# A four-layer encoder in split fp32r on one Trainium2 core: the first projections take low-rank and value columns of four feature tiles together, and of four apart

## The chip, the core and the metric

The kernel runs on one core of one Trainium2 chip, as one program with one launch. The metric is the device time of that program in microseconds, the median of several executions. The engines that matter are TensorE (PE for matmuls, PEld for the loading of their stationary operands), VectorE (DVE), ScalarE (ACT), GpSimd (POOL) and SyncE, whose queue (SPq) issues nearly all transfers from device memory.

## The reference

The input is one sequence of 256 tokens with 1024 features. Layer 0 has two groups of heads behind one input projection, and only this projection is touched by the change:

```python
def even_mixer(xn, w_in, rpb, q_norm, w_uq, kv_norm, w_ukv, w_o, cos_r, sin_r):
    hcat = xn @ w_in                       # 1024 -> 512 q, 512 k, 512 v, 256 c_q, 128 c_kv, 32 k_pe
    a_qkv = hcat[..., :o0].reshape(b, s, 3, NA_HEADS, HEAD_DIM)
    out_a = neighbourhood_attention(a_qkv[:, :, 0], a_qkv[:, :, 1], a_qkv[:, :, 2], rpb)
    c_q = rms_norm(hcat[..., o0:o1], q_norm)
    c_kv = rms_norm(hcat[..., o1:o2], kv_norm)
    k_pe = apply_rope(hcat[..., o2:][:, :, None, :], cos_r, sin_r)
    q = (c_q @ w_uq).reshape(...)          # second stage of the low-rank heads
    kv = (c_kv @ w_ukv).reshape(...)
    out_b = dense_attention(q, k, v, (MLA_NOPE + MLA_ROPE) ** -0.5)
    return jnp.concatenate([out_a, out_b], axis=-1) @ w_o

for layer in range(2):
    xn = rms_norm(x, norm_mix[layer])
    x = x + (even_mixer if layer == 0 else odd_mixer)(xn, ...)
    x = x + square(relu(rms_norm(x, norm_mlp[layer]) @ w1)) @ w2
return rms_norm(x, norm_final)
```

Layer 1 has dilated-window attention, and each layer ends in an MLP with 4096 hidden features. All arithmetic is fp32.

## The kernel before, in words

**Three passes for a product.** TensorE multiplies in fp32r, and each operand is cut into a high and a low half: `split` casts to the high half on ACT (L173) and takes the difference as the low half on DVE (L174). A product is then three matmuls, high by high, high by low and low by high (`mm3`, L177 to L179). All weights pass through this: `load_weight` brings a raw tile of up to 1 MB by SPq into one of four buffers (`raw`), `split_piece` cuts a quarter of it into `whi` and `wlo` (three buffers each), and `weight()` hands the halves to a product while it asks for four loads and two splits ahead.

**The input.** `x` holds the features transposed: eight feature tiles (`KT`) of 128 features on the partitions, 256 tokens beside. `prepare(k, ...)` multiplies tile `k` with its gain and cuts it into the pair `xh`, `xl` (ACT L213, DVE L214). The division by the norm is left until behind the products: `square_steps` (L220 to L224) sums squares, `rstd` turns them by one matmul (`columns`, L231), an addition on DVE (`ms`, L233) and a power on POOL (L239) into one factor for each token, and `diagonal` spreads it.

**The first products (`even`).** In the beginning SPq alternates a piece of `x` (128 KB) with a piece of the low-rank weights `w_c` (208 KB, 416 columns of one feature tile), eight times; then come three pieces of `w_v` (512, 512 and 1024 KB, the value columns), two 1 MB tiles of `w_qk` (queries and keys of two heads each), four small tables for the rotation and the low-rank gains (`small_loads`), and the rest. PE first runs eight matmuls on zeros (`keep_warm`), and then:

- the low-rank products of all eight feature tiles `k` for both token tiles `t`, 48 matmuls of 416 columns into two accumulators `pc` (`c_product`);
- the value products, first tiles 0 to 3 of both token tiles, then tiles 4 to 7, 48 matmuls of 512 columns (`v_steps`), with `columns` between;
- the first query and key product `qk_steps(0)` (48 matmuls of 256 columns), in the middle of it `as_row`, which lays the token factors along a row;
- `turn_c[0]`, three transposes of the normalised low-rank rows `cn` of token tile 0 (L516); the first quarter of `qk_steps(1)`; `turn_c[1]`, the same for token tile 1; the rest of `qk_steps(1)`.

`c_tail` makes those `cn`: sums of squares on ACT (L504), then for each of the two parts `ss` (L505), a power on POOL (`rsqrt`, L204), a product (L507) and the scaling (L508). The stretch up to the value products stands in the order in which it is written (`manual_schedule`); what follows is ordered by the scheduler of the tile framework.

**Attention of layer 0.** A list of main steps (the query and key products 1 to 3, the second low-rank stage, the output projection) is woven with the steps of the attention: `scores(n)` (L186 for the first group), the softmax (`sn` and its minimum `mn` on DVE, L677; the exponential on ACT, L682; the reciprocal, L683; the scaling, L685), `turn_probs` (transposes, L692) and `mix` (L706). Each of the first eight `scores` adds a bias of 256 KB (`load_bias`, two buffers), so a bias can be fetched only when the softmax two steps before has read its own.

Of the kernel before, what the change touches and what calls it, by code (L numbers as in the profile page):

```python
# [44 lines left out]
def trunk(ctx, tc, a, out):  # L45
# [32 lines left out]
    x = act.tile([P, KT, T], F32, name="x")  # L78
# [38 lines left out]

    plan("w_c", 4 * 416)
# [16 lines left out]
    def load_weight(pieces=1, before=lambda i: None):  # L135
        j = state["loaded"]
        src, n = specs[j]
        raw = wraw.tile([P, WCH], F32, tag="raw", name="raw")
        for i in range(pieces):
            c = cut(j, i, pieces)  # L140
            before(i)
# [316 lines left out]
    def even(ep):  # L458
        xT = xh, xl, _ = pair_tile()
        for j in range(2):  # L460
            load_weight(4, lambda i: nc.sync.dma_start(x[:, 4 * j + i, :], a["x"][:, 4 * j + i, :]))
        load_weight(2)
        load_weight()
# [6 lines left out]
        def small_loads():  # L470
# [3 lines left out]
            nc.sync.dma_start(gc[:, 256:384], a["kv_norm"].partition_broadcast(P))  # L474

# [16 lines left out]
        def c_product(pc, wc, k, t):  # L492
            wh, wl = wc
            ws = slice((k % 4) * 416, (k % 4) * 416 + 416)
            mm3(pc[:, 0:416], xh[:, k, tok(t)], xl[:, k, tok(t)], wh[:, ws], wl[:, ws], k == 0, k == KT - 1)

        def c_tail(t, pc):
            rt = column(r, t)
            cn = scratch([384], "cn")
            for c0, c1, tg in ((0, 256, "q"), (256, 384, "c")):  # L500
                n = c1 - c0
                ss = work.tile([P, 1], F32, tag="ss" + tg, name="ss")
                junk = scratch([n], "junk")
                nc.scalar.activation(junk, pc[:, c0:c1], AF.Square, scale=rt, accum_out=ss)  # L504
                nc.vector.tensor_scalar(ss, ss, 1.0 / n, EPS, ALU.mult, ALU.add)  # L505
                rc = rsqrt(ss, tg)
                nc.vector.tensor_tensor(rc, rc, rt, op=ALU.mult)  # L507
                nc.vector.scalar_tensor_tensor(cn[:, c0:c1], pc[:, c0:c1], rc, gc[:, c0:c1], ALU.mult, ALU.mult)  # L508
# [11 lines left out]
        def v_steps(t):  # L520
            hold = []

            def step(ks):
                if not hold:
                    hold.append(bank("acc"))
                for k in ks:
                    if t == 0 and k % 4 == 0:
                        wv.append(weight())
                    wh, wl = wv[k // 4]
                    ws = slice((k % 4) * 512, (k % 4) * 512 + 512)  # L530
                    mm3(hold[0], xh[:, k, tok(t)], xl[:, k, tok(t)], wh[:, ws], wl[:, ws], k == 0, k == KT - 1)
                return hold[0]
            return step

# [3 lines left out]
        wc, wv = [], []  # L538
        pc = [bank("acc") for _ in range(NT)]
        s = sum_tile()  # L540
        with tc.manual_schedule(engines={ENG.PE, ENG.Activation, ENG.DVE}):
            for k in range(KT):
# [4 lines left out]
                if k % 4 == 0:  # L547
                    wc.append(parts[k // 4][1:])
                for t in range(NT):
                    c_product(pc[t], wc[k // 4], k, t)  # L550
            state["used"] = 2
            del parts[0], parts[1]
            ins = [split_piece() for _ in range(WPARTS)][-1]
# [493 lines left out]
```

## Time and profile before

| what | value |
|---|---|
| median of 3 runs (lowest, highest) | 758.24 us (757.81, 758.55) |
| the profiled execution: its time | 758.64 us |
| the profiled execution: span of its records | 756.9 us |
| PE busy | 747.0 us (99%) |
| PEld busy | 688.3 us (91%) |
| DVE busy | 524.8 us (69%) |
| ACT busy | 512.7 us (68%) |
| POOL busy | 9.9 us (1%) |
| mean DMA rate over the span | 171 GB/s |
| first matmul on data starts at | 4.73 us |
| first query and key product starts at | 28.26 us |

How to read it: all times of the profile are in microseconds from the start of the span, "mean ns" is of one instruction. Matmuls are pipelined, so their durations overlap: what a matmul costs PE is the distance from its start to the next start, not its duration. A line of the timeline gives the start, the duration (of the whole group, where it says x2 or more), the engine, the source line, the operation, output and inputs with shapes, and in brackets the idle time of that engine before it with what ended it. "waits" sums such idle times: who waited, for whom, us in total, times, longest.

### The profile page before, as it was taken

The numbers are of one execution on the slowest core, as the hardware profiler recorded it, in microseconds if no ns is written. First come the engines' busy times: TensorE is split into PE (matmuls) and PEld (weight loads), VectorE is DVE, ScalarE is ACT, GpSimd is POOL, SyncE is SP. The second block draws the span as 40 slices with busy tenths as digits, with TensorE's granted clock in tenths as the row PEclk, the third lists the DMA queues.
The fourth block names the chain that finished last, engine by engine and source line by source line (L and its number), as shares of the span: only waits on it lengthen the run. The fifth ranks groups of instructions, "written<-read, shape, count | busy, mean of one in ns | idle before, by whom it ended". The sixth has DMA issues, their size and how long they took to land.

```text
span 756.9 us, 13681 instructions
## 1 busy us (share of the span) xinstructions
PE 747.0 (99%) x5386; PEld 688.3 (91%) x5386; DVE 524.8 (69%) x1091; ACT 512.7 (68%) x1111; POOL 9.9 (1%) x22
## 2 busy tenths in 40 slices
PE   8999999999999999999999999999999999999996
PEld 6888899999999999999999999999998888888885
DVE  5878858856656657886686677776759766566664
ACT  6779966545445545888989889889967554554551
POOL 0100000000000001000000000000000000000000
PEclk9999999999999999999999999999999999999998
DMA  8854334555455544643444444434554464554501
GB/s 299 293 209 155 112 112 146 189 193 185 179 186 187 185 148 179 224 153 125 162 161 154 154 139 168 155 139 158 219 196 167 166 223 167 178 211 171 192 29 55
DMA packets 22816, 129.08 MB, mean 171 GB/s; under 512 B 2912, under 2 KB 5472, under 8 KB 9824
## 3 DMA queue, kind: packets, MB, share of 16 engines
q1 hardware_dynamic: 22464, 127.94, 47.4%
q8 instruction: 42, 0.69, 0.4%
q10 hardware_dynamic: 288, 0.28, 0.1%
q14 instruction: 22, 0.18, 0.1%
HBM read 127.16 MB, written 1.05 MB: 169 GB/s over the span
## 4 chain that ended last, share of the span: by engine, by line
PE 90%; DVE 3%; DMA 2%; issue 1%; ACT 1%; POOL 1%; SPq 1%; POOLq 0%; DVEq 0%
PE acc L177 19%; PE acc L179 19%; PE acc L178 19%; PE w L341 16%; PE w L342 8%; DVE wlo L174 2%; PE w L881 1%; PE w L186 1%; PE w L861 1%; DMA raw<-in_w_v 1%; PE w L692 1%; PE w L706 1%; DMA bias<-in_rpb 1%; PE acc L891 1%; DMA raw<-in_w_c 1%
## 5 line engine op out<-in xcount | busy, mean ns | idle before, releaser
L174 DVE TENSOR_TENSOR wlo<-raw,whi 128x512 fp32r<-128x512 f32 (+3 forms) x488 | 307.5, 663 | 145.7 <-ACT whi L173 145.3
L173 ACT CAST whi<-raw 128x512 fp32r<-128x512 f32 (+3 forms) x488 | 266.2, 601 | 143.7 <-PE w L341 61.7
L341 PE MATMUL w<-pair,whi 128*128 128x512 f32 x512 | 181.3, 395 | 0.0
L342 PE MATMUL w<-pair,wlo 128*128 128x256 f32 x512 | 143.2, 280 | 0.0
L177 PE MATMUL acc<-pair,whi 128*128 128x256 f32 x432 | 125.4, 290 | 0.0
L179 PE MATMUL acc<-pair,wlo 128*128 128x256 f32 x432 | 121.9, 282 | 0.0
L178 PE MATMUL acc<-pair,whi 128*128 128x256 f32 x432 | 121.4, 281 | 0.0
L341 PEld LDWEIGHTS w<-pair,whi 128*128 128x128 f32 x512 | 96.1, 188 | 22.3
L342 PEld LDWEIGHTS w<-pair,wlo 128*128 128x128 f32 x512 | 96.1, 188 | 0.5
L177 PEld LDWEIGHTS acc<-pair,whi 128*128 128x128 f32 x432 | 81.1, 188 | 1.3 <-issue 0.3
L178 PEld LDWEIGHTS acc<-pair,whi 128*128 128x128 f32 x432 | 81.9, 189 | 0.0
L179 PEld LDWEIGHTS acc<-pair,wlo 128*128 128x128 f32 x432 | 81.2, 188 | 0.0
L179 PE MATMUL acc<-hh,wlo 128*128 128x256 f32 x256 | 72.4, 283 | 0.0
L177 PE MATMUL acc<-hh,whi 128*128 128x256 f32 x256 | 72.4, 283 | 0.0
L178 PE MATMUL acc<-hl,whi 128*128 128x256 f32 x256 | 72.4, 283 | 0.0
L177 PE MATMUL acc<-whi,pair 128*128 128x384 f32 (+2 forms) x160 | 56.4, 352 | 0.5 <-ACT whi L173 0.5
L178 PE MATMUL acc<-wlo,pair 128*128 128x384 f32 (+2 forms) x160 | 55.4, 346 | 0.4 <-DVE wlo L174 0.3
L179 PE MATMUL acc<-whi,pair 128*128 128x384 f32 (+2 forms) x160 | 55.0, 344 | 0.0
L177 PEld LDWEIGHTS acc<-hh,whi 128*128 128x128 f32 x256 | 49.0, 191 | 0.6
L179 PEld LDWEIGHTS acc<-hh,wlo 128*128 128x128 f32 x256 | 49.0, 191 | 0.0
L178 PEld LDWEIGHTS acc<-hl,whi 128*128 128x128 f32 x256 | 49.0, 191 | 0.0
L177 PE MATMUL acc<-whi,hh 128*128 128x512 f32 x122 | 47.9, 393 | 0.0
(207 smaller groups left out, 1247.7 us busy)
## 6 DMA issues: line engine op xcount, KB each, us to landing
raw<-in_w SPq DMA_DIRECT2D x64, 1024.0 KB, 4.8
raw<-in_w_oqk SPq DMA_DIRECT2D x24, 1024.0 KB, 4.8
raw<-in_w_ov SPq DMA_DIRECT2D x16, 768.0 KB, 4.3
raw<-in_w_qk SPq DMA_DIRECT2D x4, 1024.0 KB, 10.1
raw<-in_w_oe SPq DMA_DIRECT2D x4, 1024.0 KB, 6.9
raw<-in_w_oo SPq DMA_DIRECT2D x4, 1024.0 KB, 4.8
bias<-in_rpb SPq DMA_DIRECT2D x8, 256.0 KB, 4.7
raw<-in_w_c SPq DMA_DIRECT2D x8, 208.0 KB, 4.3
```

What stands on the lines that cost most here:

```text
L173: a = nc.scalar.copy(hi, src).ins
L174: return a, (eng or nc.vector).tensor_tensor(lo, src, hi.bitcast(F32), op=ALU.subtract).ins
L177: nc.tensor.matmul(o, sh, mh, start=first, stop=False)
L178: nc.tensor.matmul(o, sh, ml, start=False, stop=False)
L179: nc.tensor.matmul(o, sl, mh, start=False, stop=last)
L186: nc.tensor.matmul(o[j], y[pb, 0, ts], z[pb, 1, :], start=n == 0, stop=n == 2)
L341: nc.tensor.matmul(two(pu[f]), w[0][:, c], xT[2][:, k], start=k == 0, stop=False)
L342: nc.tensor.matmul(pu[f][:, 0:T], w[1][:, c], xT[0][:, k, :], start=False, stop=k == KT - 1)
L692: nc.tensor.transpose(pt[:, b * P:(b + 1) * P], pp[:, b // 2, (b % 2) * P:(b % 2 + 1) * P], ident)
L706: nc.tensor.matmul(pvo[64 * j:64 * j + 64, 0:P], v[:, kk, h * 64:(h + 1) * 64], pts[:, 2 * j + kk, :], start=kk == 0, stop=kk == NT - 1)
L861: nc.tensor.matmul(ss[i][j][rows, T:T + P], d["q12"][:, j, i * P + 64 * c:i * P + 64 * c + 64], d["k12"][:, j, 2 * i + c, :], start=True, ...
L881: nc.tensor.transpose(pt[:, b * P:(b + 1) * P], pp[:, b * P:(b + 1) * P], ident)
```

## The change

- **Layout of the weights and of x.** The low-rank and value columns of feature tiles 0 to 3 are joined in one array `w_cv` (two tiles of two features, 928 columns each); `w_c` and `w_v` keep feature tiles 4 to 7. The gains, before a transfer of their own on ACT's queue, stand ahead of `x` in one array `gx`.
- **Transfers.** The first ones on SPq are now `gx` with the gains and tile 0 (144 KB), `w_cv` 416 columns (208 KB), `w_cv` 512 columns (256 KB), `x` tile 1, again 208 and 256 KB, `x` tiles 2 and 3 together (256 KB), `w_cv` of features 2 and 3 in pieces of 464 KB, `x` 4 and 5, `w_c` of 4 and 5 (416 KB), `x` 6 and 7, `w_c` of 6 and 7. The four small tables come next, ahead of `w_v` (two halves of 512 KB) and of the four tiles of `w_qk`.
- **Order of the products.** Feature tiles 0 to 3: 6 matmuls of 416 columns and then 6 of 512 columns for each. Tiles 4 to 7: 6 matmuls of 416 columns. Then the values of tiles 4 to 7, token tile 0 and then token tile 1. For tile 0 both token tiles take one pass after another. Four accumulators (two `pc`, two `pv`) are open at once. The numbers of matmuls and their shapes stay.
- **Splits.** They are cut along the pieces. For tile 0 the high half of the low-rank columns is copied on DVE, not on ACT. The squares are summed within the loop. The splits of `w_v` and of the first `w_qk` follow directly behind (`split_piece` eight times), ahead of the norm's factors.
- **c_tail.** The two parts share one `ss`, one power and one product; the factor `1/n` goes into a scale `rs` for each part.
- **keep_warm** has seven matmuls, not eight.

```diff
-    keep_warm(8)
-    gains = const.tile([P, 4 * KT], F32, name="gains")
-    nc.scalar.dma_start(gains, a["gains"])
+    keep_warm(7)
...
-        for j in range(2):
-            load_weight(4, lambda i: nc.sync.dma_start(x[:, 4 * j + i, :], a["x"][:, 4 * j + i, :]))
-        load_weight(2)
-        load_weight()
+        load_weight((0, 416, CV, CV + 416, 2 * CV), lambda i: load_x(i // 2) if i % 2 == 0 else None)
+        load_weight((0, CV, 2 * CV), lambda i: load_x(2, 2) if i == 0 else None)
+        load_weight((0, 2 * 416, 4 * 416), lambda i: load_x(4 + 2 * i, 2))
...
+        small_loads()
+        load_weight((0, WCH // 2, WCH))
+        load_weight()
...
+            ss = work.tile([P, 2], F32, tag="ssc", name="ss")
+            for i, (c0, c1) in enumerate(cuts):
+                nc.scalar.activation(junk, pc[:, c0:c1], AF.Square, scale=rs[:, i, t:t + 1], accum_out=ss[:, i:i + 1])
+            nc.vector.tensor_scalar(ss, ss, EPS, None, ALU.add)
+            nc.gpsimd.tensor_tensor(rc, ss, mhalf.broadcast_to([P, 2]), op=ALU.pow)
+            nc.vector.tensor_scalar(rc, rc, rt, None, ALU.mult)
...
             for k in range(KT):
                 upper, lower = prepare(k, 0, xT)
                 upper()
-                lower()
-                split_piece()
...
+                if k == 0:
+                    nc.vector.tensor_copy(wc[1], wc[0])
+                    lower()
+                    nc.vector.tensor_tensor(wc[2], wc[0], wc[1].bitcast(F32), op=ALU.subtract)
+                else:
+                    lower()
+                    split(wc[1], wc[2], wc[0])
+                if wv:
+                    split(wv[1], wv[2], wv[0])
+                if k in (3, 5, 6, 7):
+                    squares.pop(0)()
+                for w, ps_, n in ((wc, pc, 416), (wv, pv, 512)):
+                    if w is not None:
+                        for passes in ((0,), (1,), (2,)) if k == 0 else (range(3),):
+                            for t in range(NT):
+                                product(ps_[t], n, w, k, t, passes)
+            state["split"] = 3 * WPARTS
+            for i in range(2 * WPARTS):
                 split_piece()
...
+            for t in range(NT):
+                for k in range(4, KT):
+                    product(pv[t], 512, [z[:, k - 4] for z in wv], k, t)
+                    if (t, k) == (0, 5):
+                        r = rstd(s)
```

The written order shows in three places. The first is SPq behind the pieces of the low-rank weights, where the small tables and the next weights stand. Before:

```order
L142 DMA raw<-in_w_c 128x416
L142 DMA raw<-in_w_v 128x1024 x2
L142 DMA raw<-in_w_v 128x2048
L142 DMA raw<-in_w_qk 128x2048 x2
L471 DMA cosr<-in_cos_r 128x64
L472 DMA sinr<-in_sin_r 128x64
L473 DMA gc<-in_q_norm 128x256
L474 DMA gc<-in_kv_norm 128x128
L142 DMA raw<-in_w_qk 128x2048 x2
```

And now:

```order
L84 DMA gx<-in_gx 128x512
L148 DMA raw<-in_w_cv 128x928 x2
L84 DMA gx<-in_gx 128x512
L148 DMA raw<-in_w_c 128x832
L84 DMA gx<-in_gx 128x512
L148 DMA raw<-in_w_c 128x832
L476 DMA cosr<-in_cos_r 128x64
L477 DMA sinr<-in_sin_r 128x64
L478 DMA gc<-in_q_norm 128x256
L479 DMA gc<-in_kv_norm 128x128
L148 DMA raw<-in_w_v 128x1024 x2
L148 DMA raw<-in_w_qk 128x2048 x4
```

The four tables moved ahead of `w_v` and of all `w_qk`, and the pieces ahead of them are larger and fewer.

The second place is DVE behind the first token tile's `c_tail`, up to the rows `cn` of token tile 1 that `turn_c[1]` transposes. `wlo_396` (before) and `wlo_379` (now) are the low halves of the second `w_qk`, `wlo_478` and `wlo_461` those of the third. Before:

```order
L505 TENSOR_SCALAR ss_352<-ss_352 128x1
L507 TENSOR_TENSOR rstd_356<-rstd_356,rstd_290 128x1
L508 SCALAR_TENSOR_TENSOR cn_351<-acc_133,rstd_356,gc_128 128x256
L174 TENSOR_TENSOR wlo_478<-raw_301,whi_477 128x512 x2
L505 TENSOR_SCALAR ss_360<-ss_360 128x1
L507 TENSOR_TENSOR rstd_364<-rstd_364,rstd_290 128x1
L508 SCALAR_TENSOR_TENSOR cn_351<-acc_134,rstd_364,gc_128 128x128
```

And now:

```order
L180 TENSOR_TENSOR wlo_379<-raw_372,whi_378 128x512
L515 TENSOR_SCALAR ss_347<-ss_347 128x2
L180 TENSOR_TENSOR wlo_461<-raw_374,whi_460 128x512
L518 TENSOR_SCALAR rstd_353<-rstd_353,rstd_294 128x2
L520 SCALAR_TENSOR_TENSOR cn_346<-acc_133,rstd_353,gc_118 128x256
L520 SCALAR_TENSOR_TENSOR cn_346<-acc_133,rstd_353,gc_118 128x128
```

Two rounds of `ss`, power and product became one, and one low half of the third `w_qk` stands ahead of `cn`, not two. Between `ms` and this `cn` there were ten low halves of `w_qk` before, four of them of the first tile; now there are five, since the first tile's four stand ahead of `ms`.

The third place is DVE at the first softmax, whose `sn` reads the first bias and so lets the third bias be fetched. `wlo_573` (before) and `wlo_556` (now) are the low halves of the fourth `w_qk`. Before:

```order
L174 TENSOR_TENSOR cl_130<-w_500,ch_129 128x3x128
L174 TENSOR_TENSOR wlo_573<-raw_393,whi_572 128x512 x4
L585 TENSOR_TENSOR q32_544<-acc_487,both_125 128x512
L677 ISA sn_559,mn_560<-w_550,bias_418 128x256
L677 ISA mn_560 128x1
L677 ISA sn_559,mn_560<-w_551,bias_418 128x256
L677 ISA mn_560 128x1
L174 TENSOR_TENSOR qk_l_543<-q32_544,qk_h_542 128x512
```

And now:

```order
L180 TENSOR_TENSOR cl_129<-w_483,ch_128 128x3x128
L608 TENSOR_TENSOR q32_527<-acc_470,both_115 128x512
L700 ISA sn_542,mn_543<-w_533,bias_401 128x256
L700 ISA mn_543 128x1
L700 ISA sn_542,mn_543<-w_534,bias_401 128x256
L700 ISA mn_543 128x1
L180 TENSOR_TENSOR qk_l_526<-q32_527,qk_h_525 128x512
L180 TENSOR_TENSOR wlo_556<-raw_376,whi_555 128x512
L706 RECIPROCAL rz_545<-z_544 128x2
L180 TENSOR_TENSOR wlo_556<-raw_376,whi_555 128x512 x3
```

The four low halves moved from ahead of the first `sn` to behind it. On SPq the fetch of the third bias stands one place earlier too, ahead of the second tile of the output weights and no longer behind it.

More of the change, by code (lines that the diff above doesn't have):

```diff
@@ L138, in load_weight @@
         raw = wraw.tile([P, WCH], F32, tag="raw", name="raw")
[L139 to L141 removed]
+        edges = edges or (0, n)
+        for i, c in enumerate(slice(*e) for e in zip(edges, edges[1:])):
+            earlier(i)
             nc.sync.dma_start(raw[:, c], src[:, c])
@@ L570, in even @@
+            dg = [diagonal(r, t) for t in range(NT)]
+            turn_c = [c_tail(t, pc[t]) for t in range(NT)]
+            state["used"] = 4
+            for j in range(4):
+                del parts[j]
+            for t in range(NT):
+                v_out(t, pv[t])
         qk = {}
```

95 lines of the change are left out of this document (39 added, 56 removed).

## The prediction, as put on record

> **What bounds the kernel now.** I read the page's first line, then the waits of TensorE over the whole span:
>
> ```profile
> PE 747.0 (99%) x5386; PEld 688.3 (91%) x5386; DVE 524.8 (69%) x1091; ACT 512.7 (68%) x1111; POOL 9.9 (1%) x22
> ...
> PE w L186 <- DVE obl L174: 0.6, 1, 0.6
> PE acc L177 <- ACT whi L173: 0.5, 1, 0.5
> PE w L692 <- ACT pp L685: 0.5, 1, 0.5
> PE w L516 <- DVE cn L508: 0.4, 1, 0.4
> PE acc L178 <- DVE wlo L174: 0.3, 2, 0.2
> ```
>
> TensorE is the bound, and its waits look small. But matmuls overlap, so idle time hides inside modelled durations. The timeline of PE, read by starts, shows more; the stretch is the one the change rewrites:
>
> ```profile
> 1.19 3.59 PE L87 MATMUL acc<-warm 128*128 128x512 bf16 x8 [1.19 <-DVE warm L82]
> 4.73 0.71 PE L177 MATMUL acc<-whi,pair 128*128 128x416 f32 x1
> ...
> 7.08 0.45 PE L177 MATMUL acc<-whi,pair 128*128 128x416 f32 x1 [0.51 <-ACT whi L173]
> 7.70 0.45 PE L178 MATMUL acc<-wlo,pair 128*128 128x416 f32 x1 [0.17 <-DVE wlo L174]
> ...
> 9.31 0.35 PE L177 MATMUL acc<-whi,pair 128*128 128x416 f32 x1
> ...
> 11.56 0.35 PE L177 MATMUL acc<-whi,pair 128*128 128x416 f32 x1
> ...
> 16.23 0.40 PE L177 MATMUL acc<-whi,pair 128*128 128x512 f32 x1
> ...
> 18.69 0.39 PE L177 MATMUL acc<-whi,pair 128*128 128x512 f32 x1
> ...
> 21.50 0.39 PE L177 MATMUL acc<-whi,pair 128*128 128x512 f32 x1
> ...
> 28.26 0.28 PE L177 MATMUL w<-pair,whi 128*128 128x256 f32 x1
> ```
>
> From 9.31 to 11.56 lie 12 matmuls of 416 columns: 0.188 us each, so 48 need 9.0. They take 11.5 (4.73 to 16.23): 2.5 us idle. From 18.69 to 21.50 lie 12 of 512 columns: 0.234 each, so 48 need 11.2. They take 12.0 (16.23 to 28.26); of the 0.8 left I put half to the column matmuls, which stay, and half to waits. What they wait for shows on ACT, which casts as the pieces land:
>
> ```profile
> 4.87 0.51 ACT L213 ACTIVATE pair<-x,gains 128x256 fp32r<-128x256 f32 x1 [0.20 <-DMA x<-in_x]
> 6.49 0.54 ACT L173 CAST whi<-raw 128x416 fp32r<-128x416 f32 x1 [1.11 <-DMA raw<-in_w_c]
> ...
> 11.36 0.54 ACT L173 CAST whi<-raw 128x416 fp32r<-128x416 f32 x1
> ...
> 13.94 0.54 ACT L173 CAST whi<-raw 128x416 fp32r<-128x416 f32 x1 [0.95 <-DMA raw<-in_w_c]
> ```
>
> These are tile 1 of x (480 KB asked for so far, the gains included), and the low-rank pieces of tiles 1, 6 and 7 (688, 2368 and 2704 KB). So pieces land at (2368 - 688)/4.87 = 345 KB/us at best and (2704 - 688)/7.45 = 271 KB/us with the late last one. A low-rank tile brings 336 KB for 1.13 us of PE, some 300 KB/us: as much as lands, so every late piece is idle time. With its values a tile brings 592 KB for 2.53 us, 234 KB/us. That is what the regrouping alters. The last view is of windows (busy time of PE, PEld, DVE, ACT, POOL, clock, share of the transfer engines, GB/s), for the queue and for the load of DVE and ACT:
>
> ```profile
> 14.00:15.00 1.00, 0.98 (x4) 0.37 (x2) 0.49 (x1) 0.48 (x1) 0.00 (x0) 1.00 1.05 434
> 22.00:23.00 1.00, 1.00 (x8) 0.91 (x7) 1.00 (x3) 1.00 (x3) 0.00 (x0) 1.00 1.04 285
> 23.00:24.00 1.00, 1.00 (x6) 0.82 (x5) 1.00 (x3) 0.99 (x2) 0.00 (x0) 1.00 0.92 187
> 24.00:25.00 1.00, 1.00 (x6) 0.77 (x6) 0.10 (x2) 0.06 (x1) 0.71 (x1) 1.00 1.02 165
> 80.00:90.00 10.00, 10.00 (x85) 8.91 (x85) 9.27 (x31) 9.82 (x29) 0.00 (x0) 1.00 0.29 107
> ```
>
> **The change part by part.** *Tile 0.* Its first matmul can start only when `whi` exists. The copy on DVE runs beside ACT's pair, and seven warm-up matmuls of 0.44 us end by about 4.3, so the start moves from 4.73 to between 4.2 and 4.8. This is worth nothing by itself, because the values of tile 0 gate the next six matmuls: they are the 608th KB, between 480 KB (4.87) and 688 KB (6.49), so 5.9. Cast 0.6, six matmuls 1.4: tile 0 ends at 7.9. The low half is done by 7.1, ahead of its pass.
>
> *Tile 1.* Low-rank weights at 944 KB: 6.49 + 256/345 = 7.2, cast by 7.8, in time for 7.9. With the low half late by 0.2, as at 7.70, PE ends at 7.9 + 2.53 + 0.2 = 10.65.
>
> *Tile 2.* Its weights are one piece of 464 KB that must land whole, at 1920 KB: 6.49 + 1232/345 = 10.1 or, by the slower rate, 11.0. With 0.6 for the cast, PE starts at 10.65 to 11.6. I take 10.95, nearer to the fast rate, because rows of 2 KB and more move faster than the 1 and 1.6 KB ones now (434 GB/s at 14, when rows of 4 and 8 KB of `w_v` move).
>
> *The rest of the products.* From tile 2 on PE needs 12 x 0.188 + 12 x 0.234 + 24 x 0.188 + 24 x 0.234 = 15.2, the column matmuls 0.4 and a late low half 0.2: 15.8. So the first query product starts at 26.7 (26.4 to 27.4) instead of 28.26: **1.5 us won (0.85 to 1.85)**.
>
> *DVE, which must follow.* These rows are of DVE, POOL and one of PE:
>
> ```profile
> 9.53 0.48 DVE L214 SCALAR_TENSOR_TENSOR pair<-x,gains,pair 128x256 fp32r<-128x256 f32 x1
> 10.46 0.48 DVE L214 SCALAR_TENSOR_TENSOR pair<-x,gains,pair 128x256 fp32r<-128x256 f32 x1
> 15.97 2.57 DVE L174 TENSOR_TENSOR wlo<-raw,whi 128x512 fp32r<-128x512 f32 x4 [0.86 <-ACT whi L173]
> 18.82 2.29 DVE L222 TENSOR_TENSOR squares<-squares,q 128x512 f32<-128x512 f32 x3 [0.28 <-ACT q L220]
> 23.89 0.15 DVE L233 TENSOR_SCALAR ms<-w 128x2 f32<-128x2 f32 x1
> 27.98 0.92 POOL L204 TENSOR_TENSOR rstd<-ss,mhalf 128x1 f32<-128x1 f32 x1 [3.07 <-DVE ss L505]
> 28.93 0.16 DVE L507 TENSOR_TENSOR rstd<-rstd 128x1 f32<-128x1 f32 x1 [0.43 <-POOL rstd L204]
> 36.64 0.35 DVE L508 SCALAR_TENSOR_TENSOR cn<-acc,rstd,gc 128x128 f32<-128x128 f32 x1
> 37.05 0.33 PE L516 MATMUL w<-ident,cn 128*128 128x128 f32 x1 [0.45 <-DVE cn L508]
> ```
>
> The last low-rank piece (3728 KB) lands at 6.49 + 3040/345 = 15.3, or 17.7 by the slower rate. Behind it DVE has a cast to wait for (0.6), two pairs with low halves (0.93 each, 9.53 to 10.46), two squares (0.76 each) and their fold (half as wide, 0.4): 19.7 or 22.1. Then come four low halves of the values and four of the first `w_qk` (2.5 us each four). `ms`, now behind both, is at T = 24.7 to 27.1; I take 25.5. Before, the last `cn` was done 13.1 us behind `ms` (23.89 to 36.99). Five low halves fewer stand between (3.1), two rounds over POOL fewer (0.43 idle to 0.92 power each; 0.65 taken, so 1.3), and the scales `rs` are new (0.2): T + 8.9 = 34.4. PE asked for it at 36.6, which is 8.3 behind 28.26, so it asks at 35.0. The wait of 0.45 goes while T stays under 26.1: **0.35 won**, with a rest kept. If T is 27.1 and PE on time, it costs 1.0.
>
> PE needs the first `w_qk` from 26.7 on at 0.7 us for a quarter, DVE makes one in 0.62 and starts on them at T - 2.5 = 23.0: covered by some 3 us. The other small edits (gains without a transfer of their own, one `ss`, one product) lie on ACT and DVE beside PE and cost nothing while these margins hold; without them DVE would be late for `turn_c[1]` by what they add, under 0.5 us.
>
> *The third bias.* PE, DVE and SPq around the first two softmaxes:
>
> ```profile
> 41.62 0.39 PE L186 MATMUL w<-qk_h 64*128 64x256 f32 x2
> 43.91 0.41 DVE L677 CUSTOM_DVE_ANT_0 sn<-w,bias 128x256 f32<-128x256 f32 x1
> 44.70 3.11 SPq L657 DMA_DIRECT2D bias<-in_rpb  x2
> 50.91 0.42 DVE L677 CUSTOM_DVE_ANT_0 sn<-w,bias 128x256 f32<-128x256 f32 x1 [1.88 <-DMA bias<-in_rpb]
> 53.82 0.84 PE L692 MATMUL w<-ident,pp 128*128 128x128 f32 x4 [0.49 <-ACT pp L685]
> ```
>
> The chain is: first `sn` (2.3 us behind the first scores at 41.62, because four low halves of `w_qk` stand ahead of it), fetch of the third bias (44.70), landing (50.9), third softmax, PE's wait of 0.49. Now those low halves stand behind `sn`: it comes some 0.9 us behind the scores, the fetch 1.4 us earlier against PE. That is more than 0.49, so this wait goes: **0.49 won**. What is late next is DVE itself, which then has those four halves to make up (PE needs them only for the fourth product).
>
> Sum: 1.53 + 0.35 + 0.49 = 2.4 us. The profiled execution took 758.64 us, of which 756.9 are its span; 758.64 - 2.4 = 756.25, and it stood 0.4 above the median, so the runs should come to **755.9**.
>
> **A rule against this.** The eight warm-up matmuls take 0.44 us for 512 columns where later ones take 0.234: half speed. From 9.31 on, behind a gap of 0.5 us, the full speed is there. The change takes one warm-up away, and opens gaps of some 0.4 us in tile 0. The Trainium skill, TensorE: Matmul & The Clock Gate, Part 1: The HAM clock gate, says that the array stays at half clock until a free-running window of about 3.4 us has seen sustained work. By that rule the clock could rise one window later here; the trace has the half-speed warm-up of some 3.5 us, and no run yet shows which gaps are too many.
>
> **The rivals.** (1) *The clock rises late.* Tile 0 at half speed: 6 x 0.36 + 6 x 0.44 = 4.8 us from 4.5, so 9.3 instead of 7.9; with 2.73 for tile 1, tile 2 starts at 12.0, 1.1 later, of which 0.1 is not waited for at `cn`: 756.9. For it: the row of 1.19. Against: idle 0.51 at 7.08 did no harm.
>
> (2) *The large pieces land late*, by the slower rate: tile 2 at 11.6, so PE is 0.65 late and asks for `cn` at 35.7; T = 27.1 gives it at 36.0, a wait of 0.3 for 0.45: 0.85 + 0.15 + 0.49 = 1.5 won, 756.7, on the edge of what can be told. For it: 13.94.
>
> (3) *The tables come in front.* With the transfer engines as busy as at 14, the windows have only 285, 187 and 165 GB/s from 22 to 25; I read this as the tables, which then come up in the queue. At 212 instead of 434 GB/s these 3 us lose 1.5. Now the tables stand ahead of `w_v` and the first `w_qk`, so T may be 26.1 to 28.5. Each us of T above 26.1 stops PE for one at `turn_c[1]`. The gain is used up at T = 28.5, and the kernel is slower by more than 0.2% from T = 30.1 on. That needs a dip twice as long on top of the slow rate, T = 30.5: 760.0. Against it: the products still have 10 us to run when the tables are asked for.
>
> (4) *The gain is given back* in the attention, where ACT (9.82 of 10) and DVE (9.27) are nearly full from 80 to 90: PE comes earlier, and waits there: 758.0. Against it: PE's one long wait behind 60 us is 0.6.
>
> **How the numbers follow.** 0.2% (1.5 us) is about what a measurement of this kernel can tell from no change, so faster means under 756.7 and slower over 759.8. The forecast holds 0.64 (own range 754.4 to 756.6; the lower end is all idle time gone, 2.5 + 0.4 + 0.45 + 0.49 = 3.8); the late clock 0.09; late pieces 0.12, counted half as faster; tables 0.08, of which 0.05 slower; given back 0.06; 0.01 slower for what I do not see. The range 754.3 to 757.5 takes in (1) and (2) and what lies up to half-way to (4); it leaves out (3). Faster 0.64 + 0.06 = 0.70, same 0.09 + 0.06 + 0.03 + 0.06 = 0.24, slower 0.06.
>
> **What would show it.** Right: tile 2's first matmul near 11, the first query product near 26.7, no wait on `cn`, the third `sn` without a wait for its bias. Wrong: half-speed spacing (0.36) in tile 0; the cast of tile 2 behind 11.6; `ms` behind 27; new waits of PE between 55 and 95.

## The result and the profile after

The changed kernel takes 753.3 us (median of 6 runs, 752.65 to 753.97), the kernel before 758.14 in the same session (757.72 to 758.55): ratio 0.9937, interval 0.9924 to 0.995. That is 4.8 us faster, where 2.2 to 2.4 had been forecast, and it lies below the forecast's range. The profiled spans are 751.7 us after and 756.9 before; they lie 5.2 apart because the profiled execution before (758.64) stood 0.5 above its median.

The page's first line and the waits of TensorE, changed kernel (who waited, for whom, us in total, times, longest):

```profile
PE 741.5 (99%) x5385; PEld 680.8 (91%) x5385; DVE 523.4 (70%) x1089; ACT 512.3 (68%) x1111; POOL 8.7 (1%) x20
...
PE acc L184 <- DVE wlo L180: 1.1, 4, 0.3
PE w L192 <- DVE obl L180: 0.6, 1, 0.6
PE acc L505 <- ACT whi L179: 0.5, 1, 0.5
PE w L528 <- DVE cn L520: 0.3, 1, 0.3
```

TensorE is still the bound. The wait on `pp` (the third bias) is gone, the one on `cn` is smaller, and a new one on `wlo` stands in the odd layer. Now the rows that answer to the forecast's start, PE first and then the engines that it waits for:

```profile
4.38 1.39 PE L505 MATMUL acc<-whi,pair 128*128 128x416 f32 x4
5.98 1.09 PE L505 MATMUL acc<-whi,pair 128*128 128x512 f32 x4
7.37 0.54 PE L505 MATMUL acc<-whi,pair 128*128 128x416 f32 x2
10.51 0.64 PE L505 MATMUL acc<-whi,pair 128*128 128x416 f32 x2 [0.46 <-ACT whi L179]
26.46 0.28 PE L183 MATMUL w<-pair,whi 128*128 128x256 f32 x1
34.53 0.52 PE L528 MATMUL w<-ident,cn 128*128 128x128 f32 x3 [0.27 <-DVE cn L520]
```

```profile
4.52 0.62 ACT L179 CAST whi<-raw 128x512 fp32r<-128x512 f32 x1 [1.15 <-DMA raw<-in_w_cv]
9.91 1.06 ACT L179 CAST whi<-raw 128x416 fp32r<-128x416 f32 x2 [1.51 <-DMA raw<-in_w_cv]
25.28 0.15 DVE L239 TENSOR_SCALAR ms<-w 128x2 f32<-128x2 f32 x1
33.90 0.74 DVE L520 SCALAR_TENSOR_TENSOR cn<-acc,rstd,gc 128x256 f32<-128x256 f32 x2
39.79 0.41 DVE L700 CUSTOM_DVE_ANT_0 sn<-w,bias 128x256 f32<-128x256 f32 x1
45.85 0.42 DVE L700 CUSTOM_DVE_ANT_0 sn<-w,bias 128x256 f32<-128x256 f32 x1
```

Tile 0's values land at 4.5, tile 2's weights at 9.9, `ms` is done at 25.3, and the third `sn` (45.85) follows without a wait for its bias. All steps of the forecast are there, and together they are worth about what it said. The rest lies elsewhere, and only a count shows it. The next rows are windows of 18 us within the odd layer's first query and key products, where PE runs nothing but products of 256 columns with `pair` streamed and a weight stationary (busy time and instructions of PE, PEld, DVE, ACT, POOL, clock, share of the transfer engines, GB/s). Before, and after:

```profile
314.00:332.00 18.00, 18.00 (x152) 18.00 (x152) 13.68 (x24) 15.95 (x32) 0.00 (x0) 1.00 0.46 157
```

```profile
310.00:328.00 18.00, 18.00 (x161) 18.00 (x161) 14.38 (x25) 16.74 (x33) 0.00 (x0) 1.00 0.44 155
```

PE is busy for all 18 us in both, at the same clock, and does 152 matmuls in one and 161 in the other. Over the whole stretch (168 recorded products, from the first start to the last) a product starts 120.5 ns behind the one ahead before and 113.9 ns after: 20.12 us against 19.03. No line of the diff touches this stretch. So 1.1 us of the gain are made here, some 250 us behind the last place that the edits touch.

What the change moved there are addresses. In the built program the small tiles of the work pool take 96 bytes less per partition (`c_tail` has one `ss` and one `rstd` of two buffers where it had two each, 128 bytes less; `rs` takes 32). Whatever is allocated behind them, `raw`, `whi`, `wlo` and the tiles of each layer, slid down by 96: `whi` starts at 122,240, which is 128 modulo 256, where it was at 122,336, which is 224. `pair` stayed at 26,944, which is 64. The distance from `pair` to `whi`, modulo 256, went from 160 to 64.

### The profile page after: what moved, and what is told of

Read it like the earlier page. It is cut to its first block, busy times and chain, and to the rows that moved or that the text cites. A ratio compares the mean times of both kernels' runs of the same rounds, so it can differ in the third digit from the quotient of the medians.

```text
span 751.7 us, 13661 instructions
## 1 busy us (share of the span) xinstructions
PE 741.5 (99%) x5385; PEld 680.8 (91%) x5385; DVE 523.4 (70%) x1089; ACT 512.3 (68%) x1111; POOL 8.7 (1%) x20
## 4 chain that ended last, share of the span: by engine, by line
PE 66%; ACT 17%; DVE 10%; issue 4%; DMA 2%; SPq 0%; POOL 0%; POOLq 0%
PE w L347 16%; PE acc L183 12%; PE acc L184 12%; PE acc L185 12%; PE w L348 8%; ACT whi L179 6%; DVE wlo L180 4%; ACT sw L845 3%; ACT sw L844 3%; ACT v L822 1%; DVE r L847 1%; ACT pp L895 1%; DVE sw L848 1%; DVE k L857 1%; DVE sn L893 1%
## 5 line engine op out<-in xcount | busy, mean ns | idle before, releaser
L183 PE MATMUL acc<-pair,whi 128*128 128x256 f32 x432 | 123.5, 286 | 0.0
L185 PE MATMUL acc<-pair,wlo 128*128 128x256 f32 x432 | 120.2, 278 | 0.0
L184 PE MATMUL acc<-pair,whi 128*128 128x256 f32 x432 | 120.0, 278 | 0.0
L185 PE MATMUL acc<-whi,hl 128*128 128x512 f32 x122 | 47.6, 390 | 0.0
L184 PE MATMUL acc<-wlo,hh 128*128 128x512 f32 x122 | 47.6, 390 | 0.0
L184 PE MATMUL acc<-wlo,pair 128*128 128x384 f32 x128 | 44.0, 344 | 1.2 <-DVE wlo L180 1.1
```

The lines of the kernel that those rows point to most:

```text
L183: nc.tensor.matmul(o, sh, mh, start=first, stop=False)
L184: nc.tensor.matmul(o, sh, ml, start=False, stop=False)
L185: nc.tensor.matmul(o, sl, mh, start=False, stop=last)
```

## The experiments

Theory A: the addresses make up what the forecast lacked. Rival B: the rewritten start brings all of it by a mechanism that I overlooked. The fifteen kernels, each beside runs of the kernel before on the same chip (spacing: mean from start to start of such products over all thirty stretches with 24 or more of them in a row, without the intervals over 160 ns, where a record is missing or a stretch begins; 119.9 ns before, 114.4 in the changed kernel). The rows 1 to 4, 5 to 8, 9 to 12 and 13 to 15 were each measured together with the column "before us", and the changed kernel's 753.30 together with 758.14; where rows of different groups are compared, the ratio is the safer number:

| | kernel | median us | before us | ratio (interval) | spacing ns |
|---|---|---|---|---|---|
| 1 | before, weights at 128 | 756.06 | 757.86 | 0.9975 (0.9966 to 0.9984) | 114.5 |
| 2 | changed, weights at 224 | 755.49 | 757.86 | 0.9965 (0.9952 to 0.9979) | 119.9 |
| 3 | changed, weights at 160 | 751.80 | 757.86 | 0.9915 (0.9902 to 0.9929) | 117.8 |
| 4 | changed, weights at 0 | 753.60 | 757.86 | 0.9942 (0.9929 to 0.9954) | 117.1 |
| 5 | changed, distance 160 | 755.78 | 758.49 | 0.9965 (0.9952 to 0.9977) | 119.9 |
| 6 | changed, weights at 224, distance 64 | 752.98 | 758.49 | 0.9930 (0.9917 to 0.9942) | 113.7 |
| 7 | changed, hh and hl 64 ahead of whi | 751.90 | 758.49 | 0.9916 (0.9902 to 0.9930) | 114.4 |
| 8 | as 3, hh and hl 96 ahead of whi | 752.32 | 758.49 | 0.9920 (0.9908 to 0.9932) | 117.8 |
| 9 | as 3, hh and hl moved in the first mlp alone | 750.67 | 757.76 | 0.9907 (0.9893 to 0.9920) | 118.0 |
| 10 | changed, without the regrouping | 755.37 | 757.76 | 0.9969 (0.9958 to 0.9981) | 114.3 |
| 11 | changed, w_qk's splits left to the program | 753.56 | 757.76 | 0.9948 (0.9935 to 0.9960) | 115.1 |
| 12 | changed, one warm-up matmul | 753.91 | 757.76 | 0.9949 (0.9936 to 0.9963) | 114.5 |
| 13 | changed, gains apart | 754.67 | 758.13 | 0.9954 (0.9942 to 0.9967) | 114.6 |
| 14 | changed, distance 128 | 754.82 | 758.13 | 0.9957 (0.9944 to 0.9971) | 118.7 |
| 15 | changed, distance 32 | 754.51 | 758.13 | 0.9954 (0.9942 to 0.9967) | 118.3 |

**1 to 4: the place of the weights.** One unused tile is laid between the pools:

```diff
+    gap = ctx.enter_context(tc.tile_pool(name="gap", bufs=1)).tile([P, 40], F32, name="gap")   # 40, 24, 8, 32 numbers
     wraw = ctx.enter_context(tc.tile_pool(name="wraw", bufs=RAWBUFS))
...
     nc.gpsimd.memset(mean, 1.0 / D)
+    nc.gpsimd.memset(gap, 0.0)
```

> The kernel before with 160 unused bytes per partition between the small work tiles and the raw weights, so that whi, wlo and all behind them lie at 128 modulo 256, as in the changed kernel, instead of 224; nothing else differs. Theory A (addresses: products that stream pair against stationary whi or wlo go at 114 ns from start to start instead of 120 because the weights lie 96 bytes lower): about half of the gain of 4.8 us, so 755.3 to 756.0, with those products at 113 to 115 ns. Rival B (the regrouped start alone brings 4.8, by a mechanism that I overlooked, and the faster products belong to it): 758.1, products at 120 ns.

> The changed kernel with 96 unused bytes per partition at the same place, so that whi, wlo and all behind lie at the very addresses of the kernel before. Theory A: 755.5 to 756.2, the forecast 755.9 being right for the rest of the change, products of pair against whi at 120 ns from start to start. Rival B: 753.3, products at 114 ns.

> The changed kernel with 32 unused bytes there: weights at 160 modulo 256, which is 32 modulo 64 as before. Theory A1 (the weights must lie at a multiple of 64 bytes): as slow as at 224, 755.5 to 756.2, 120 ns. Theory A2 (something else about the place, a distance of 128 or less from pair's 64 modulo 256): 753.3, 114 ns. Rival B: 753.3.

> The changed kernel with 128 unused bytes there: weights at 0 modulo 256, a multiple of 64. Theory A1 (multiple of 64 bytes): 753.3, 114 ns. Theory A2 (128 is a special place): 755.5 to 756.2, 120 ns. Rival B: 753.3.

The same window in kernel 1 and in kernel 2:

```profile
312.50:330.50 18.00, 18.00 (x161) 18.00 (x161) 14.44 (x25) 16.76 (x33) 0.00 (x0) 1.00 0.45 159
```

```profile
311.00:329.00 18.00, 18.00 (x153) 18.00 (x152) 13.66 (x23) 15.95 (x32) 0.00 (x0) 1.00 0.46 158
```

Rival B falls. The old code at the new addresses has the 161 matmuls and wins 1.8 us; the new code at the old addresses has the 153 and comes to 755.49, 2.4 below its own before. The two gains, 1.8 and 2.4, add up to 4.2 of the 4.8, and their ratios multiply to 0.9940 against 0.9937. Kernel 1 lies 0.06 above its range and kernel 2 0.01 below. A multiple of 64 bytes is not the rule (A1): kernel 3, at 160, is the fastest of the four, and kernel 4, at 0, has 117 ns. Both have a spacing between the 114 and the 120 that all expectations for them knew, so A2 missed as well.

**5 and 6: place or distance.** In both an unused tile stands ahead of `pair`, of 160 bytes (with 96 more at the first place) and of 96.

```diff
+    low = act.tile([P, 40], F32, name="low")      # kernel 5; 24 in kernel 6
```

> The changed kernel with 160 unused bytes ahead of pair and 96 between the small work tiles and the raw weights. The weights stay at 128 modulo 256, and pair goes from 64 to 224, so that the weights lie 160 bytes behind pair modulo 256, as in the kernel before. Theory A3 (what counts is the distance between the streamed and the stationary operand): products of pair against whi at 120 ns, 755.2 to 756.0. Theory A4 (what counts is the place of the weights alone): 114 ns, 753.0 to 753.6.

> The changed kernel with 96 unused bytes ahead of pair: pair goes from 64 to 160 and the weights from 128 to 224 modulo 256, so the weights lie where they were before, and their distance to pair is the 64 of the changed kernel. Theory A3 (distance): 114 ns, 753.0 to 753.6. Theory A4 (place of the weights): 120 ns, 755.2 to 756.0.

The window in kernel 5 and in kernel 6:

```profile
310.50:328.50 18.00, 18.00 (x153) 18.00 (x152) 13.62 (x24) 15.97 (x31) 0.00 (x0) 1.00 0.44 157
```

```profile
310.00:328.00 18.00, 18.00 (x161) 18.00 (x161) 14.47 (x25) 16.76 (x33) 0.00 (x0) 1.00 0.45 157
```

Weights at the good place and `pair` moved away from them: 153. Weights at the place of before and `pair` moved along: 161. So it is the distance between the two operands (A3), not the place of the weights (A4), and kernel 1, whose distance is 256 bytes larger than the changed kernel's, shows that it counts modulo 256 or a divisor of it. Kernels 5 and 6 ran together and differ by 2.8 us (kernel 6 lies 0.02 below its range). The Trainium skill, TensorE: Matmul & The Clock Gate, Part 2 (What happens when you issue a matmul), says that PE has two independent read ports, and that loading the next weights takes no read bandwidth from the running matmul. From that alone one would not expect it to matter where the two lie; in these runs it does, by 6 ns in 120, and the measurement decides. Through which part of the hardware, no run here shows.

**7 to 9: the other streamed operands.** In the first mlp `hh` and `hl` are streamed past `whi`. They and the weights had moved together by 96, and their 120 ns had stayed. An unused tile between pools moves all that lies behind it; the new one here moves the layers' own tiles, `hh` and `hl` among them, but neither `pair` nor the weights, and in kernel 9 the first mlp's pool alone.

```diff
+    high = ctx.enter_context(tc.tile_pool(name="high", bufs=1)).tile([P, 48], F32, name="high")   # 7; in 8, 40 numbers, with the gap of 3
...
     def mlp_between(mp, xT, s):
+        nc.gpsimd.memset(mp.tile([P, 40], F32, name="off"), 0.0)                                   # 9 alone, with the gap of 3
```

> The changed kernel with 192 unused bytes behind the split weights, so that hh and hl (the first layer's other streamed operands) go from 128 to 64 modulo 256 and lie 64 bytes ahead of whi modulo 256, as pair does; pair and the weights stay. Theory A3 (distance): products of hh and hl against whi go from 120 to 114 ns; 760 of them would save 4.6 us if nothing else bounds the stage, so 749 to 752.5. Theory A4 (place of the weights): 753.0 to 753.6, 120 ns.

> The changed kernel with 32 unused bytes in front of the raw weights and 160 behind the split ones: weights at 160 modulo 256 as in the third kernel (751.8 us), hh and hl at 64 instead of 160. Theory A3 (distance): the products of hh and hl go from 120 to 117 ns, so 749.5 to 751. Theory A4 (place of the weights): 751.5 to 752.1.

> The changed kernel with 32 unused bytes in front of the raw weights (weights at 160 modulo 256) and 160 at the head of the first layer's mlp pool alone, so that its hh and hl lie at 64 there, as in the eighth kernel, while hh and hl of the last layer stay where the third kernel has them. It takes from each stage the distance that was fastest there. Theory A3 (distance, stage by stage): 751.8 less the 1.8 us that the eighth kernel won in the first mlp (163.04 against 164.83), so 749.7 to 750.5. Rival (what one stage wins the next gives back, as in the odd layer): 751.5 to 752.0.

The first mlp's length, from its first product of `hh` to its last, is 166.13 us in the changed kernel and 164.71 in kernel 7; it is 164.83 in kernel 3, and 163.04 and 163.03 in 8 and 9, which are made from it. A window of 150 us there, in the changed kernel and in kernel 9:

```profile
140.00:290.00 150.00, 150.00 (x1062) 140.63 (x1061) 93.20 (x161) 72.73 (x143) 0.00 (x0) 1.00 0.51 180
```

```profile
140.00:290.00 150.00, 150.00 (x1086) 141.52 (x1086) 95.46 (x165) 74.22 (x146) 0.00 (x0) 1.00 0.53 187
```

The products of `hh` went to a median of 117 to 118 ns in kernels 7 and 8, so distance works for a second pair of operands; but not to 114, and kernel 7 won 1.4 us where up to 4.6 was allowed. Kernel 8 missed its 749.5 to 751: in the last mlp `hh` is the stationary operand and `whi` the streamed one, 512 columns wide, and there the shift took the products from 227 to between 231 and 237 ns, which gives back 1.9 us (157.70 to 159.65 from the first of these products to the last). Kernel 9 leaves the last mlp alone and is the fastest here, 750.67: 7.1 us below its before. It missed its 749.7 to 750.5 by 0.2.

**14 and 15: the slope.** The first edit with 16 and 56 numbers.

> The changed kernel with 64 unused bytes in front of the raw weights: weights 128 bytes behind pair modulo 256. If the spacing rises steadily with the distance from 64 on (114 at 64, 117 at 96, 120 at 160): 118 to 119 ns, and 752.5 to 755. If 64 and 96 are single good places: 120 ns and 755 to 756.

> The changed kernel with 224 unused bytes in front of the raw weights: weights 32 bytes behind pair modulo 256. If the spacing falls off to both sides of 64: 116 to 118 ns, and 752 to 754.5. If 64 and 96 are single good places: 120 ns and 755 to 756.

By distance from `pair` to `whi`, the mean spacing is 118.3 ns (32), 114.4 (64), 117.8 (96), 118.7 (128), 119.9 (160) and 117.1 (192). So 64 is no single good place; the spacing rises on both sides of it, and steeply. Both times lie where a slope from 64 would put them (754.51 on its edge, with a spacing 0.3 above the expected 116 to 118). Since 64 and 192 differ, no smaller power of two than 256 will do. Within a stretch the rate is constant, and it is one of a few: at 160 all thirty stretches have 119.7 to 120.0; in the changed kernel 23 have 113.3 to 114.1 and seven have 117.8; at 192, six have 113.3 and 24 have 117.8; kernel 6, at 64 like the changed one, has only the fast rate. The distance sets which rates can come, and what chooses between them is open. The distance of 64 is not the best for every shape. The wide products of both mlps (512 columns of `pair` against `whi`), as groups of changed kernel and kernel 3 (in all us, mean ns of one, idle before):

```profile
L347 PE MATMUL w<-pair,whi 128*128 128x512 f32 x512 | 182.3, 398 | 0.0
```

```profile
L349 PE MATMUL w<-pair,whi 128*128 128x512 f32 x512 | 179.2, 392 | 0.0
```

From start to start in the first mlp they take 234.5 ns on the mean at 32, 235.1 at 64, 229.2 at 96, 230.6 at 128, 233.0 at 160 (the kernel before) and 231.0 at 192, without one interval of some 420 ns in each. In the last mlp the same holds within 0.5 but for 32, where they take 230.7; so the distance alone does not settle it. That is why kernel 3, slower in the narrow products, is faster than the changed kernel: its two mlps are 1.3 and 1.5 us shorter.

**10: without the regrouping.** The order of the products and the pieces of the weights are as before, everything else as changed. The small tables stand behind all of `w_v` and ahead of all of `w_qk`, which is their place in neither kernel: before, two tiles of `w_qk` were ahead of them, so that part is not as the expectation says.

```diff
-                if k < 4:
-                    c0 = k % 2 * CV
-                    wc, wv = views(k // 2, c0, c0 + 416), views(k // 2, c0 + 416, c0 + CV)
-                else:
-                    wc, wv = views(2, (k - 4) * 416, (k - 3) * 416), None
+                wc, wv = views(k // 4, k % 4 * 416, k % 4 * 416 + 416), None
...
+            for ks in (range(4), range(4, KT)):
+                for t in range(NT):
+                    for k in ks:
+                        product(pv[t], 512, [z[:, k % 4] for z in wv[k // 4]], k, t)
```

> The changed kernel without the regrouping: low-rank products of all eight tiles first, then the values, loaded and tabled as in the kernel before; the gains in x's transfer, the one power for both parts, rs, the order of the splits and all addresses stay as changed. The forecast's first term (regrouping fills PE's waits for pieces): the first query product goes from 26.5 back to about 28.0, so 754.8 (754.2 to 755.4). Rival (the start is won by the smaller edits, such as the gains without a transfer of their own): 753.0 to 753.7, first query product before 27.

PE's first query product, `ms` and the wait for `cn` in kernel 10:

```profile
27.04 0.28 PE L181 MATMUL w<-pair,whi 128*128 128x256 f32 x1
...
27.29 0.15 DVE L237 TENSOR_SCALAR ms<-w 128x2 f32<-128x2 f32 x1
...
35.96 0.52 PE L526 MATMUL w<-ident,cn 128*128 128x128 f32 x3 [1.13 <-DVE cn L518]
```

It loses 2.1 us by the medians, at the upper end of what was expected, and the intervals of the ratios do not overlap; the profiled execution, the fastest of its six, shows 1.4 of it (span 753.1 for 751.7). They are not where they were expected: the first query product is only 0.6 later than in the changed kernel (not 1.5), and 1.13 are a wait on `cn`. Here `ms` stands behind the low halves of a `w_qk` that lands later, at T = 27.29. The forecast's line "T + 8.9" gives 36.2; PE went on at 36.0. And its remark that T = 27.1 costs 1.0 is what this run shows. That PE begins at 27.04 without regrouping, 1.2 earlier than before, must come from edits that this kernel keeps, if it is no accident of this trace: the first data product starts 0.6 earlier (4.14 for 4.73). Which edit brings how much is not shown; see 13.

**11: the order of the splits.**

```diff
-            for i in range(2 * WPARTS):
+            for i in range(WPARTS):
```

> The changed kernel in which only the values' splits follow the products by hand, and those of the first w_qk are placed by the program, after ms among the tails. The forecast's second and third terms: ms about 2.4 earlier, so no wait on cn (0.3 won), but low halves of w_qk stand in front of the first sn again, and the third bias is waited for (0.5 lost): 753.3 to 753.9. Rival (the order of these splits is worth more, because PE waits for the first w_qk's low halves, which now come between the tails): 754.0 to 755.0, with a wait of PE on wlo behind 26.5.

```profile
28.02 0.39 PE L185 MATMUL w<-pair,wlo 128*128 128x256 f32 x1 [0.40 <-DVE wlo L180]
...
22.96 0.16 DVE L239 TENSOR_SCALAR ms<-w 128x2 f32<-128x2 f32 x1 [0.71 <-PE w L237]
...
41.61 0.41 DVE L700 CUSTOM_DVE_ANT_0 sn<-w,bias 128x256 f32<-128x256 f32 x1
...
54.67 0.42 DVE L700 CUSTOM_DVE_ANT_0 sn<-w,bias 128x256 f32<-128x256 f32 x1 [1.18 <-DMA bias<-in_rpb]
```

Both sides are there, the rival's too: `ms` is 2.3 earlier and no wait on `cn` is left, PE waits 0.40 for a low half of `w_qk`, and the first `sn` comes 1.8 behind its scores (39.85) instead of 0.7. A bias is late again, the fifth and not the third, and PE does not wait for it. The sum, 753.56, is not told apart from the changed kernel's 753.30. The profiled span is longer by more, 753.1 for 751.7, but half of that is the stretch of 310, which runs at 117.8 ns here (168 products, 156 in the window that held 161):

```profile
311.00:329.00 18.00, 18.00 (x156) 18.00 (x155) 13.96 (x24) 16.22 (x32) 0.00 (x0) 1.00 0.46 163
```

**12: one warm-up matmul.** `keep_warm(1)` for `keep_warm(7)`.

> The changed kernel with one warm-up matmul instead of seven, so that PE is idle from about 1.7 to 4.4. Theory of the clock gate (full speed comes only behind some 3.5 us of work, as in the warm-up): tile 0's twelve products at half speed, 4.8 us instead of 3.0, tile 1 from about 9.2 on, tile 2 from 11.8 instead of 10.5: 754.0 to 754.8. Rival (the late pieces hide it, or the clock does not depend on the warm-up): 753.0 to 753.6, spacing of 0.19 in tile 0 or tile 2 still near 10.5.

```profile
4.21 1.72 PE L505 MATMUL acc<-whi,pair 128*128 128x416 f32 x4 [2.41 <-DVE whi L556]
5.73 0.89 PE L505 MATMUL acc<-wlo,pair 128*128 128x416 f32 x2
6.42 1.83 PE L505 MATMUL acc<-whi,pair 128*128 128x512 f32 x4
8.09 0.63 PE L505 MATMUL acc<-wlo,pair 128*128 128x512 f32 x2
8.55 0.54 PE L505 MATMUL acc<-whi,pair 128*128 128x416 f32 x2
11.33 0.65 PE L505 MATMUL acc<-whi,pair 128*128 128x416 f32 x2
```

The window of 5 to 6 us in it:

```profile
5.00:6.00 1.00, 1.00 (x4) 0.95 (x4) 0.64 (x1) 0.35 (x2) 0.00 (x0) 1.00 0.76 213
```

Tile 0 runs at half speed (six products of 416 columns from 4.21 to 6.42, four of 512 to 8.09) and then at full, so the clock rose some 3.9 us behind 4.21. In the changed kernel the warm-up starts at 1.19, and 0.20 from start to start is reached from 5.21 on, 4.0 us behind; that its first product starts 0.66 behind the last warm-up, not 0.43, did no harm. The Trainium skill, TensorE: Matmul & The Clock Gate, Part 1 (The HAM clock gate), has full speed behind about 3.4 us of work in a window that runs freely; these traces agree with somewhat more. Tile 1 starts 1.2 later and tile 2 0.8, less than expected because tile 2's weights land late anyway. The median, 753.91, lies between the two expectations; it is 0.6 us above the changed kernel's, and the intervals overlap.

**13: the gains apart.**

```diff
+    gains = const.tile([P, 4 * KT], F32, name="gains")
+    nc.scalar.dma_start(gains, a["gains"])
...
-        nc.sync.dma_start(gx[:, c], a["gx"][:, c])
+        nc.sync.dma_start(x[:, k:k + n, :], a["x"][:, k:k + n, :])
```

> The changed kernel with one of its small edits undone: the gains have a tile and a transfer of their own on ACT's queue again, and x comes without them; all addresses from pair on stay. The forecast costed this edit at nothing: 753.0 to 753.6. Theory S (the joint transfer brings the whole start forward, since the first pair on ACT starts at 2.87 instead of 3.74): first data matmul near 4.7, first query product 26.8 to 27.2, 753.7 to 754.3.

```profile
3.60 0.51 ACT L220 ACTIVATE pair<-x,gains 128x256 fp32r<-128x256 f32 x1 [0.93 <-DMA gains<-in_gains]
5.61 0.62 ACT L180 CAST whi<-raw 128x512 fp32r<-128x512 f32 x1 [1.51 <-DMA raw<-in_w_cv]
10.69 1.06 ACT L180 CAST whi<-raw 128x416 fp32r<-128x416 f32 x2 [1.39 <-DMA raw<-in_w_cv]
...
27.23 0.28 PE L184 MATMUL w<-pair,whi 128*128 128x256 f32 x1
```

The first pair waits for the small transfer to 3.60, tile 0's values land 1.1 later than in the changed kernel, tile 2's weights 0.8, and the first query product starts 0.8 later. At the end 0.5 us are left in the traces, 1.4 in the medians, above both expectations; the intervals overlap a little. Eleven kernels have the changed start as it is (the changed kernel, 2 to 9, 14 and 15). Their values of tile 0 land at 4.5 to 5.2, so 5.61 is outside. But their weights of tile 2 land anywhere from 9.16 to 10.45, and in each of them the first query product follows 16.5 to 16.7 us behind, as it does here (10.69 and 27.23). So the landing of this piece sets the start, and only 0.2 of the 0.8 lie outside what one profile differs from the next without any edit. This edit, costed at nothing, is probably worth something; how much is open.

## Why the prediction was wrong, and where it was right

**The step that failed is one that the sum does not have.** The change was worked out where its lines stand, and every other matmul was taken to keep its spacing. Among the small edits, said to cost nothing beside PE, was "one `ss`": with the new `rs` it makes a pool 96 bytes smaller, and every weight behind it moved against `pair`. That is worth 2.2 us here (kernel 2 against the changed one; 1.8 by kernel 1 against its before, 2.8 by kernels 5 and 6), about as much as all that was forecast. Nothing in a trace of before could have given its size; the addresses of the two built programs could have shown that they moved.

**Where the 2.2 us lie**, from kernel 2 to the changed one, by the distances between the same products in the two traces: 0.7 from the first query product to layer 0's first product of 384 columns (59.3 in the changed kernel), 0.4 from its output projection to the first product of `hh`, 1.1 in the odd layer's first products, 0.7 from its output projection on in the same way; the mlps lose 0.3 and 0.5. In the middle of the odd layer, from behind those first products to its last product of 384 columns, nothing is won: 207.11 us in kernel 2, 207.13 in the changed one, although its narrow products have become 4.6 us shorter in sum. The products of 384 columns, kernel 2 and changed:

```profile
L186 PE MATMUL acc<-wlo,pair 128*128 128x384 f32 x128 | 43.0, 336 | 0.0
```

```profile
L184 PE MATMUL acc<-wlo,pair 128*128 128x384 f32 x128 | 44.0, 344 | 1.2 <-DVE wlo L180 1.1
```

PE comes early there and waits for low halves; from start to start those products lose 3.3 us in sum, and transposes another 1. What paces the layer at 207 us was not tried. The forecast's rival (4), a gain given back behind the start, came true in this layer, not in the one it named, and for the gain in spacing; VectorE is busy 71% and ScalarE 90% of the time from 331 to 535 there, so "nearly full" fits only ScalarE.

**The edits themselves came out.** With the old addresses (kernel 2) the gain is 2.4 us, and the forecast was 2.4. Term by term, in the changed kernel:

- *First query product*: 26.46 (forecast 26.7, 26.4 to 27.4), 1.80 won for 1.5. The parts are less good. Tile 0's values landed at 4.5, not 5.9, tile 2 started at 10.51, a little under 10.65 to 11.6; both fit better with the gains apart (5.6 and 11.3). So part of this term may belong to the joint transfer, which was put at nothing, and not to the regrouping, whose loss moves the start by 0.6; that the sum came out is in part luck. Among the kernels with the same start the first query product lies between 25.7 and 27.0, so a few tenths of one trace say little.
- *The wait on `cn`*: `ms` at 25.28 (25.5). The wait is 0.27 instead of gone, since PE asks at 34.26, not 35.0: it starts 0.2 earlier than forecast, and its products are faster; at the old addresses (kernel 2, `ms` at 25.76) the wait is gone. The term was right, its size 0.18 of 0.35.
- *The third bias*: the first `sn` 0.7 behind its scores (39.07; forecast 0.9), the bias in time, PE's 0.49 gone. Right.

**The rivals.** The clock (1): the first products of tile 0 are at half speed up to about 5.2, as before, the rest at full; kernel 12 shows the mechanism and that six warm-ups less do not move the median measurably. Late pieces (2): tile 2's cast at 9.91, so no. The tables (3): the windows that had 285, 187 and 165 GB/s now show

```profile
22.00:23.00 1.00, 1.00 (x8) 0.88 (x7) 0.14 (x1) 0.79 (x2) 0.00 (x0) 1.00 1.01 426
23.00:24.00 1.00, 1.00 (x6) 0.81 (x5) 1.00 (x2) 1.00 (x3) 0.00 (x0) 1.00 1.07 451
24.00:25.00 1.00, 1.00 (x6) 0.84 (x5) 1.00 (x3) 0.40 (x1) 0.00 (x0) 1.00 0.98 401
```

and the one at 14, which had 434, 191: the slow transfers moved ahead with the tables, as rival (3) said, and `ms` stayed under 26.1 all the same. (By this rival's own line, one us for each us of T above 26.1, its T = 30.5 gives 760.3 and not 760.0.)

## What to carry to other kernels

When an edit changes what is allocated, compare the addresses of the big operands before and after, and where all else is settled, try a few unused bytes between the pools: here 32 bytes were worth 1.5 us over the changed kernel (1.7 by the ratios), and 192 bytes in two places 2.6 (2.3). To see such a thing in a profile, count the matmuls in equal windows of a stretch that nobody edited; busy shares and clock do not show it. A term that comes out in sum can still be put down to the wrong edit. Runs that undo one edit each are the way to see it, but one profile of each does not divide the start's 1.8 us here, since kernels with the same start differ by 1.3.

## What the hardware showed unexpectedly

- The spacing of fp32r matmuls hangs here on the distance, modulo 256 bytes, between streamed and stationary operand: 114 to 120 ns for 256 columns, 229 to 235 for 512, with the best distance of those tried not the same for both (64 and 96). At 64 and at 192 a stretch has one of two rates, 113.5 or 117.8 ns, and keeps it to its end; at 96 its rate lies between 117.2 and 120.0.
- The clock column of the windows reads 1.00 while matmuls run at half speed (kernel 12, 5 to 6 us: four matmuls of 416 columns, 0.35 apart). Half speed shows only in the distances from start to start.
- Kernels of one start differ in their first query product by up to 1.3 us from one profile to the next (25.7 to 27.0), by the landing of tile 2's weights (9.2 to 10.5).
